# First mixer: the products of hv for token tile 1 put behind the first hu and hg, and conversions for the output projection put behind the subtraction of the mean

## The chip, the cores and the metric

The kernel runs on one core of one Trainium2 chip. The metric is the device time of one execution in microseconds (us). Five engines work side by side, each on its own queue in order: PE (TensorE: matmuls, with weight loads that overlap them), DVE (VectorE), ACT (ScalarE), POOL (GpSimd) and SP (SyncE, which here only issues transfers). An instruction waits at the head of its engine's queue until what it reads or overwrites is ready, and everything behind it on that engine waits too.

## The reference, cut to what matters

Two transformer layers on 256 tokens of width 1024 in float32, and then a third, different block. Each layer is a feed-forward (`swiglu`), a mixer, and a second feed-forward, each with a normalisation before and after it and a residual sum. The change touches the first layer's mixer and, through the order of conversions, the start of the feed-forward behind it:

```python
def even_mixer(h, w_in, w_out, dw_w, dw_b, ln_g, ln_b):
    q, k, v, u, gate = split(h @ w_in)        # 512 columns each
    a_out = stick_breaking_attention(q, k, v)  # 8 heads of 64
    c = u * sigmoid(gate)
    c = causal_depthwise_conv(c, dw_w, dw_b)   # 31 taps, 512 channels
    c = silu(layer_norm(c, ln_g, ln_b))        # mean and variance over the channels
    return concat([a_out, c]) @ w_out
```

## The kernel before, in words

All 256 tokens are in SBUF, in two token tiles of 128. A float32 product is made of three products of rounded parts: high by high, high by low, low by high. So every weight chunk of 512 KB is loaded by SP into one of four raw buffers, its high part is written by ACT (line 246, tile `hi`) and its low part by DVE (line 247, tile `lo`, raw minus hi; on POOL in a few places). That pair is called a conversion here. The chunks come in one fixed list, the plan, and are numbered here by their place in it: 66 to 69 are hv, 70 and 71 the first hu, 72 and 73 the first hg, 74 to 77 the second hu and hg, 78 to 85 hq and hk in turn, 86 to 93 ho (the output projection), and 94 to 97 the four chunks with which the next feed-forward starts.

`nxt` hands out the next chunks. Before that it converts ahead: up to `depth` chunks beyond the one in use, and at most one more than it hands out. With `ahead=False` it converts no more than what it hands out. `catch_up(n)` converts up to n more. For every name that `nxt` hands out it also calls the functions in the list `side`. Every order is the order of the program text; there is no planner.

At the end of a feed-forward, `boundary` adds its result to the residual, transposes token tile 0 for the next stage, writes its parts xh and xl (`evac`, lines 418 and 419), and makes one conversion (`catch_up(CU[1])`). The mixer then takes all four hv chunks and makes the products of token tile 0 with them; in between, token tile 1 is transposed, and after that its xh and xl are written, in the order k = 0, 4, 1, 5, 2, 6, 3, 7, its norm is taken, and two conversions are made (`catch_up(CU[2])`). Then come the products of token tile 1 (24 of 512 columns). Then `wp("hu")` and `wp("hg")`, 48 products of 256 columns each over both token tiles, `nz.rows()` (the norm as a row, `rb`, line 432), and on DVE `us` (841), `sgg` (845) and, after a sigmoid on ACT, the padded convolution input `cpad` (848), two channel blocks for each pass c of the loop at line 835.

The convolution has four channel blocks of 31 taps: blocks 0 and 2 on DVE (lines 798 to 805), blocks 1 and 3 as multiplies on ACT (808 to 821) and sums on POOL (818 to 823). `conv_some` is put into `side` after pass c = 0 and runs up to six times 3 or 2 DVE taps and 3 ACT taps with the hu, hg, hq and hk that follow. `qT` (863) and `kT` (866) are evacuated by DVE behind those taps. `z_` makes logits, `e_` their softplus (DVE end: `ze`, 892), `c_` the cumulative sums, `o_` the attention output. Behind the last `e_` the remaining DVE taps finish `y`; the first `part(HL, True)` of the output projection is called; PE sums `y` for the mean (924), DVE subtracts it (926), ACT squares, PE sums again for the variance (932), and the convolution's half of the output projection's input is made.

Of the kernel before, what the change touches and what calls it, by code (L numbers as in the profile page):

```python
# [12 lines left out]
AF = mybir.ActivationFunctionType  # L13
# [23 lines left out]
DEPTH = (14, (12, 9), (10, 10), (10, 10))  # L37
# [8 lines left out]
HL = ((1, 1),)  # L46
# [142 lines left out]
def block_kernel(ctx: ExitStack, tc: tile.TileContext, a: dict, out: bass.AP, upto: int = 99):  # L189
    nc = tc.nc  # L190
    pe, act, dve, pool = nc.tensor, nc.scalar, nc.vector, nc.gpsimd
# [20 lines left out]
    def s2(shape, dt=F32, name="s2"):  # L212
        return wk.tile(shape, dt, tag="s2", name=name, bufs=NS2)
# [4 lines left out]
    pos = {"dma": 0, "cv": 0, "use": 0, "depth": DEPTH[0]}  # L218
# [32 lines left out]
    def nxt(*names, ahead=True):  # L251

        i = pos["use"]
        for d_, nm in enumerate(names):
            assert plan[i + d_][0] == nm, (plan[i + d_][0], nm)
        n = i + len(names)
        feed_cv(max(n, min(i - 1 + pos["depth"], pos["cv"] + len(names) + 1)) if ahead else n)
        pos["use"] += len(names)
        for _ in names:
            for f in list(side):  # L260
                f()
        r = [cv_t.pop(i + d_) for d_ in range(len(names))]
        return r if len(r) > 1 else r[0]

    def catch_up(n, lo_on=dve):
        feed_cv(min(pos["use"] - 1 + pos["depth"], pos["cv"] + n), lo_on)

    def mm3(o, lh, ll, rh, rl, start, stop):
        pe.matmul(o, lh, rh, start=start, stop=False)  # L269
        pe.matmul(o, lh, rl, start=False, stop=False)  # L270
        pe.matmul(o, ll, rh, start=False, stop=stop)  # L271

    def tsl(t):
        return slice(t * 128, (t + 1) * 128)
# [277 lines left out]
    def smm(o, t, ch, k0, nk, xh, xl):  # L552
        for k in range(ch[0].shape[1]):
            kk = k0 + k
            mm3(o, xh[:, kk, tsl(t)], xl[:, kk, tsl(t)], ch[0][:, k], ch[1][:, k], kk == 0, kk == nk - 1)
# [5 lines left out]
            for t in range(2):  # L561
                smm(o(t), t, ch, k0, nk, xh, xl)

    def sproj_ab(o, name, xh, xl, nk=8, mid=None):

        chs = nxt(*[name] * (nk // 2), ahead=mid is None)
        for t in range(2):
            for i, ch in enumerate(chs):
                if t == 0 and i == nk // 2 - 1 and mid:
                    mid.trans(1, [0])  # L570
                smm(o(t), t, ch, 2 * i, nk, xh, xl)
            if t == 0 and mid:
                mid.trans(1, [1])
                mid.evac(1)
                mid.scale(1)
                catch_up(CU[2])

    def sproj_tail(name, xh, xl):

        f = [[None, None], [None, None]]  # L580
        pos["depth"] = DEPTH[0]
        todo = {t: {n: [0, 1, 2, 3] for n in range(2)} for t in range(2)}
        chs = {}

        def bank(t, n):
            f[t][n] = f[t][n] or pb()
            return f[t][n]

        def one(t, n, i):
            smm(bank(t, n), t, chs[i][n], 2 * i, 8, xh, xl)  # L590

        def part(leave=(), low_last=False):

            i = len(chs)
            chs[i] = nxt(name, name)
            tn = [(t, n) for t in range(2) for n in range(2) if (t, n) not in leave]
            for t, n in tn:
                todo[t][n].remove(i)
                if not low_last:
                    one(t, n, i)  # L600
            for low in range(2 if low_last else 0):
                for t, n in tn:
                    o = bank(t, n)
                    for k in range(2):
                        kk = 2 * i + k
                        hi, lo = (z[:, k] for z in chs[i][n])
                        if low:
                            pe.matmul(o, xl[:, kk, tsl(t)], hi, start=False, stop=kk == 7)
                        else:
                            pe.matmul(o, xh[:, kk, tsl(t)], hi, start=kk == 0, stop=False)  # L610
                            pe.matmul(o, xh[:, kk, tsl(t)], lo, start=False, stop=False)

        def pieces():
            i0 = len(chs)
            cs = nxt(*[name] * (2 * (4 - i0)), ahead=False)
            for i in range(i0, 4):
                chs[i] = cs[2 * (i - i0):2 * (i - i0) + 2]
            return lambda t: [(lambda n=n, i=i: one(t, n, i)) for n in range(2) for i in todo[t][n]]
        return f, part, pieces


    mod = const.tile([128, 48], F32, name="mod")
    part = const.tile([128, 192], F32, name="part")
# [142 lines left out]
    def even_mixer(nz):  # L766
        x = nz.x
        v = s4([128, 2, 512], name="v")
        pv = pp()
        sproj_ab(lambda t: pv[t], "hv", x.h, x.l, mid=nz)  # L770
        for t in range(2):
            act.activation(v[:, t], pv[t], AF.Copy, scale=x.r[t])
        cf, cr = s2([128, 3, 128], name="cf"), s2([128, 512], F32R, name="cr")
        ntri, nones, mean1 = cf[:, 0], cf[:, 1], cf[:, 2]
        idr, zmask = cr[:, :128], cr[:, 128:]
# [51 lines left out]
        def conv_some(n=None, m=TP):  # L827
            if n is None:
                n = TD[len(calls) % len(TD)]
                calls.append(n)  # L830
            for q, n_ in ((dq, n), (aq, m)):
                for _ in range(min(n_, len(q))):
                    tap(*q.pop(0))

        for c in range(2):
            pu = wp("hu", x)
            if c == 0:
                p = wp("hg", x)
                nz.rows()
            us = s2([128, 2, S], name="us")  # L840
            dve.tensor_tensor(us, two(pu), bc2(x.rb), op=ALU.mult)
            if c:
                p = wp("hg", x)
            sg = s2([128, 2, S], name="sgg")
            dve.tensor_tensor(sg, two(p), bc2(x.rb), op=ALU.mult)
            act.activation(sg, sg, AF.Sigmoid)
            for i in range(2):
                dve.tensor_tensor(cpad[2 * c + i][:, CW - 1:], sg[:, i], us[:, i], op=ALU.mult)
            dq += [(2 * c, k, True) for k in range(CW)]
            aq += [(2 * c + 1, k, False) for k in range(CW)]  # L850
            if c == 0:
                side.append(conv_some)
        pos["depth"] = DEPTH[1][1]
        act.preload_act_table_set("natural_log_exp_and_others")
        mh, ml = x8([128, 8, S], name="mh"), x8([128, 8, S], name="ml")
# [52 lines left out]
        def o_(hp):  # L908
            w = st.pop(hp)
            po = pb()  # L910
            for i in range(2):
                o = 64 * i
                hs = slice((2 * hp + i) * 64, (2 * hp + i + 1) * 64)
                pe.matmul(po[o:o + 64, 0:256], v[:, 0, hs], w[:, i, :256], start=True, stop=False)
                pe.matmul(po[o:o + 64, 128:256], v[:, 1, hs], w[:, i, 256:], start=False, stop=True)
            act.activation(mh[:, hp], po[:, :S], AF.Copy)
            dve.tensor_tensor(ml[:, hp], po[:, :S], mh[:, hp], op=ALU.subtract)
# [11 lines left out]
        def conv_var():  # L929
            pq.append(pb())  # L930
            for c in range(4):
                pe.matmul(pq[0][:, :S], mean1, y2[:, c], start=c == 0, stop=c == 3)
            rs = s2([128, S], name="rs")
            act.activation(rs, pq[0][:, :S], AF.Ln, bias=eps)
            act.activation(rs, rs, AF.Exp, scale=-0.5)
            act.preload_act_table_set("silu_and_others")
            t = s2([128, S], name="rst")
            dve.scalar_tensor_tensor(t, in0=pq[0][:, :S], scalar=EPS, in1=rs, op0=ALU.add, op1=ALU.mult)
            dve.scalar_tensor_tensor(t, in0=t, scalar=0.5, in1=rs, op0=ALU.mult, op1=ALU.mult)
            dve.scalar_tensor_tensor(rs, in0=t, scalar=1.5, in1=rs, op0=ALU.subtract, op1=ALU.mult, reverse0=True)  # L940
            for c in range(4):
                dve.tensor_tensor(y[:, c], y[:, c], rs, op=ALU.mult)
            for c in range(4):
                act.activation(y2[:, c], y[:, c], AF.Silu, scale=cols_[:, 2, 28 + c:29 + c],
                               bias=cols_[:, 2, 32 + c:33 + c])
                split_sb(mh[:, 4 + c], ml[:, 4 + c], y2[:, c])
# [18 lines left out]
        f, part, pieces = sproj_tail("ho", mh, ml)  # L965
# [1 line left out]
        conv_some(*TC[3])  # L967
        e_(3)
        conv_some(99, 99)
        part(HL, True)  # L970
        y2 = s4([128, 4, S], name="y2")
        c_(2)
        c_(3)
        conv_mean()
        o_(2)
        o_(3)
        conv_var()
        part(HL)
        return f, pieces()
# [565 lines left out]
    nz = Lazy(gcol(0, 0))  # L1545
# [19 lines left out]
    for i in range(6):  # L1565
# [8 lines left out]
        if i < 5:  # L1574
            l2, s2_ = divmod(i + 1, 3)
            nz = Lazy(gcol(l2, 2 * s2_))
        else:
# [4 lines left out]
            nz = Shifted(A1, mod[:, 0:8], fill)  # L1582
# [9 lines left out]
    nz = Shifted(A2, mod[:, 24:32], fill)  # L1592
# [46 lines left out]
```

## Time and profile before

| what | us |
|---|---|
| median of 3 runs | 1455.03 |
| lowest and highest run | 1448.93 and 1455.91 |
| profiled execution, its own time | 1453.46 |
| its span, first to last instruction | 1451.7 |
| PE busy in the span | 1432.5 |
| DVE busy in the span | 981.4 |
| ACT busy in the span | 758.4 |
| POOL busy in the span | 249.7 |

The span is what the trace shows; the execution's own time has some 1.8 us around it. The share of busy time is an average over stages: PE's few idle stretches are where time can be won or lost, and the mixer that the change touches lies between about 201 and 317 us of the span.

### The profile page before, as it was taken

The page shows a single profiled execution, that of the slowest core. Times are in us where ns is not written, and L with a number is a line of the kernel's source. Part 1 is how long each engine was busy: PE and PEld are TensorE (multiplying, and loading weights), DVE is VectorE, ACT ScalarE, POOL GpSimd, SP SyncE. Part 2 cuts the span into 40 slices and gives each one's busy share as a digit, 9 for nine tenths or more (in the row PEclk, how much of TensorE's full clock was granted, in tenths as well). Part 3 has the DMA queues.
Part 4 walks back from the last instruction along what each step waited for, and adds up shares of the span by engine and source line. Part 5 has one row for each costly group of instructions (what it writes and reads, how often), then busy time and mean ns, then how long its engine had stood idle before and what let it go on. Part 6 is the DMA issues. An engine that isn't in the chain of part 4 may idle for free.

```text
span 1451.7 us, 24310 instructions
## 1 busy us (share of the span) xinstructions
PE 1432.5 (99%) x9591; PEld 1308.9 (90%) x9591; DVE 981.4 (68%) x1348; ACT 758.4 (52%) x1166; POOL 249.7 (17%) x311
## 2 busy tenths in 40 slices
PE   9999999999999999999999999999999999999997
PEld 8899989789999999999898999998988877899997
DVE  5777667977777577765586777755695865575542
ACT  6544456965544464443664655445643665655431
POOL 3000023901100111000253100001232230200001
PEclk9999999999999999999999999999999999999999
DMA  8888645238887478775542587763664554387540
GB/s 267 265 270 250 200 145 168 73 117 285 270 264 232 146 256 268 224 233 161 172 145 65 184 292 251 236 193 111 206 202 132 188 168 143 116 270 239 176 129 29
DMA packets 194948, 281.03 MB, mean 194 GB/s; under 512 B 12381, under 2 KB 148241, under 8 KB 194834
## 3 DMA queue, kind: packets, MB, share of 16 engines
q1 hardware_dynamic: 184386, 248.87, 54.0%
q0 software_dynamic: 10048, 30.03, 6.3%
q8 instruction: 75, 1.23, 0.3%
q10 hardware_dynamic: 400, 0.57, 0.1%
q14 instruction: 39, 0.32, 0.1%
HBM read 277.90 MB, written 1.05 MB: 192 GB/s over the span
## 4 chain that ended last, share of the span: by engine, by line
PE 88%; DVE 5%; DMA 3%; ACT 2%; issue 1%; POOL 0%; SPq 0%; POOLq 0%; DVEq 0%; ACTq 0%
PE pb L269 27%; PE pb L271 26%; PE pb L270 26%; DVE lo L247 2%; DMA raw<-in_ffn_w_in_dram 2%; DVE pb L802 2%; PE pb L694 1%; PE pb L697 1%; PE pb L693 1%; PE pb L392 1%; ACT hi L246 1%; PE pb L1118 1%; DMA raw<-in_w_in_dram 0%; DMA raw<-in_ffn_w_out_dram 0%; PE pb L520 0%
## 5 line engine op out<-in xcount | busy, mean ns | idle before, releaser
L247 DVE TENSOR_TENSOR lo<-raw,hi 128x1024 fp32r<-128x1024 f32 (+1 forms) x461 | 551.6, 1224 | 239.9 <-ACT hi L246 203.4
L246 ACT ACTIVATE hi<-raw 128x1024 fp32r<-128x1024 f32 (+1 forms) x472 | 476.8, 1036 | 216.3 <-PE pb L271 68.1
L269 PE MATMUL pb<-xh,hi 128*128 128x256 f32 x1968 | 559.3, 284 | 2.7 <-DVE u L754 2.6
L271 PE MATMUL pb<-xh,lo 128*128 128x256 f32 x1968 | 557.8, 283 | 0.0
L270 PE MATMUL pb<-xl,hi 128*128 128x256 f32 x1968 | 557.8, 283 | 0.0
L269 PEld LDWEIGHTS pb<-xh,hi 128*128 128x128 f32 x1968 | 377.3, 192 | 6.0 <-issue 3.0
L270 PEld LDWEIGHTS pb<-xl,hi 128*128 128x128 f32 x1968 | 377.2, 192 | 2.0
L271 PEld LDWEIGHTS pb<-xh,lo 128*128 128x128 f32 x1968 | 377.3, 192 | 0.2
L269 PE MATMUL pb<-hi,hh 128*128 128x512 f32 x440 | 172.1, 391 | 0.0
L270 PE MATMUL pb<-lo,hh 128*128 128x512 f32 x440 | 171.8, 390 | 0.0
L271 PE MATMUL pb<-hi,hl 128*128 128x512 f32 x440 | 171.3, 389 | 0.0
L636 POOL DMA_DIRECT2D ada<-in_w_ada_dram x96 | 51.6, 541 | 455.2 <-PE pb L271 272.3
L527 ACT ACTIVATE hh<-u 128x512 fp32r<-128x512 f32 x50 | 31.6, 632 | 134.3 <-DVE u L754 134.3
L271 PEld LDWEIGHTS pb<-hi,hl 128*128 128x128 f32 x440 | 82.6, 188 | 17.5
L269 PEld LDWEIGHTS pb<-hi,hh 128*128 128x128 f32 x440 | 82.8, 188 | 15.8
L270 PEld LDWEIGHTS pb<-lo,hh 128*128 128x128 f32 x440 | 82.8, 188 | 15.4
L269 PE MATMUL pb<-hi,xh 128*128 128x512 f32 x224 | 90.8, 405 | 0.5 <-ACT xh L473 0.4
L271 PE MATMUL pb<-hi,xl 128*128 128x512 f32 x224 | 87.6, 391 | 0.0
L270 PE MATMUL pb<-lo,xh 128*128 128x512 f32 x224 | 87.4, 390 | 0.0
L739 ACT ACTIVATE sg<-sg 128x512 f32<-128x512 f32 x40 | 25.3, 632 | 111.8 <-DVE sg L738 111.8
L641 DVE SCALAR_TENSOR_TENSOR adacc<-ada,sc,adacc 128x512 f32<-128x512 f32 x84 | 63.0, 750 | 2.0
L754 DVE TENSOR_TENSOR u<-sg,pb 128x512 f32<-128x512 f32 x50 | 34.1, 682 | 40.3 <-PE pb L271 39.5
(322 smaller groups left out, 1652.2 us busy)
## 6 DMA issues: line engine op xcount, KB each, us to landing
raw<-in_ffn_w_in_dram SPq DMA_DIRECT2D x176, 512.0 KB, 5.1
raw<-in_ffn_w_out_dram SPq DMA_DIRECT2D x88, 512.0 KB, 4.6
raw<-in_w_in_dram SPq DMA_DIRECT2D x56, 512.0 KB, 4.1
ada<-in_w_ada_dram POOLq DMA_DIRECT2D x96, 256.0 KB, 4.4
raw<-in_gla_w_in_dram SPq DMA_DIRECT2D x24, 512.0 KB, 4.6
raw<-in_w_ffn_gate_dram SPq DMA_DIRECT2D x22, 512.0 KB, 4.6
raw<-in_w_ffn_up_dram SPq DMA_DIRECT2D x22, 512.0 KB, 4.9
raw<-in_w_ffn_down_dram SPq DMA_DIRECT2D x22, 512.0 KB, 4.1
```

Of the source, the lines that this page charges most:

```text
L246: act.activation(hv, r, AF.Copy)
L247: lo_on.tensor_tensor(lv, r, hv, op=ALU.subtract)
L269: pe.matmul(o, lh, rh, start=start, stop=False)
L270: pe.matmul(o, lh, rl, start=False, stop=False)
L271: pe.matmul(o, ll, rh, start=False, stop=stop)
L392: pe.transpose(nz.p[i][:, k * 128:(k + 1) * 128], h[:, t, c0:c0 + 128], ident)
L527: act.activation(hi, full, AF.Copy)
L636: pool.dma_start(t, w_ada[kt * 128:(kt + 1) * 128, cb * 512:(cb + 1) * 512])
L641: dve.scalar_tensor_tensor(ada["acc"], in0=t, scalar=sc[:, kt:kt + 1], in1=ada["acc"], op0=ALU.mult, op1=ALU.add)
L739: act.activation(sg, sg, AF.Silu)
L754: dve.tensor_tensor(u, sg, two(pb_), op=ALU.mult)
L802: dve.scalar_tensor_tensor(o, in0=src, scalar=w, in1=o, op0=ALU.mult, op1=ALU.add)
```

## The change: what it does

The mixer makes hv's products of token tile 0 as before, stops there, and makes those of token tile 1 only after the first hu, the first hg and the norm's row (`hv1()`). From the stop until then `depth` is 7. The convolution's first 5 DVE taps and 4 ACT taps are issued by themselves as soon as `cpad` 0 and 1 are made, and the two evacuations of v come behind them. At the mixer's end the first `part` of the output projection is called with `ahead=False`, so it converts nothing beyond what it uses, and one `catch_up(1)` is put behind `o_(3)`.

```diff
-    def sproj_ab(o, name, xh, xl, nk=8, mid=None):
+    def sproj_ab(o, name, xh, xl, nk=8, mid=None, later=False):
...
                 catch_up(CU[2])
+                if later:
+                    break
+
+        def rest():
+            for i, ch in enumerate(chs):
+                smm(o(1), 1, ch, 2 * i, nk, xh, xl)
+        return rest
...
-        def part(leave=(), low_last=False):
+        def part(leave=(), low_last=False, ahead=True):
             i = len(chs)
-            chs[i] = nxt(name, name)
+            chs[i] = nxt(name, name, ahead=ahead)
...
-        sproj_ab(lambda t: pv[t], "hv", x.h, x.l, mid=nz)
-        for t in range(2):
-            act.activation(v[:, t], pv[t], AF.Copy, scale=x.r[t])
+        hv1 = sproj_ab(lambda t: pv[t], "hv", x.h, x.l, mid=nz, later=True)
+        pos["depth"] = 7
...
                 p = wp("hg", x)
                 nz.rows()
+                hv1()
+                pos["depth"] = DEPTH[1][0]
...
             if c == 0:
                 side.append(conv_some)
+                conv_some(5, 4)
+                for t in range(2):
+                    act.activation(v[:, t], pv[t], AF.Copy, scale=x.r[t])
...
-        part(HL, True)
+        part(HL, True, False)
...
         o_(2)
         o_(3)
+        catch_up(1)
         conv_var()
         part(HL)
```

## Rows read from the trace of the kernel before

**Rows 1.** Page, busy us of an engine, share of the span, instructions.

```profile
PE 1432.5 (99%) x9591; PEld 1308.9 (90%) x9591; DVE 981.4 (68%) x1348; ACT 758.4 (52%) x1166; POOL 249.7 (17%) x311
```

**Rows 2.** Busy time by stretch: PE, PEld, DVE, ACT, POOL, clock, DMA share, GB/s.

```profile
278.00:290.00 12.00, 10.23 (x52) 7.26 (x52) 11.47 (x26) 11.87 (x23) 11.24 (x10) 1.00 0.00 0
```

**Rows 3.** PE's waits over the whole span: us, times, longest.

```profile
PE pb L269 <- DVE u L754: 2.6, 1, 2.6
...
PE pb L932 <- ACT y L927: 0.7, 1, 0.7
PE pb L875 <- DVE kT L866: 0.6, 1, 0.6
```

**Rows 4.** Timeline of PE: start, length, line, operation, tiles, count, wait before.

```profile
210.61 0.48 PE L269 MATMUL pb<-hi,xh 128*128 128x512 f32 x1
...
216.68 0.28 PE L269 MATMUL pb<-xh,hi 128*128 128x256 f32 x1
...
228.19 0.38 PE L430 MATMUL pb<-ident,rs_y 128*128 128x128 f32 x2
...
257.19 0.52 PE L871 MATMUL pb<-cr 128*128 128x384 f32 x2
...
281.31 1.53 PE L608 MATMUL pb<-hi,ml 128*128 128x512 f32 x6
...
291.64 1.99 PE L924 MATMUL pb<-y,cf 128*128 128x256 f32 x8 [0.22 <-DVE y L805]
```

**Rows 5.** Timeline of DVE up to the first convolution input.

```profile
213.65 0.35 DVE L419 SCALAR_TENSOR_TENSOR xl<-pb,cols,xh 128x128 fp32r<-128x128 f32 x1 [0.17 <-ACT xh L418]
...
230.31 0.42 DVE L432 COPY rb<-pb 128x256 f32<-128x256 f32 x1
...
234.09 0.76 DVE L848 TENSOR_TENSOR cpad<-sgg,us 128x256 f32<-128x256 f32 x2 [2.04 <-ACT sgg L846]
```

**Rows 6.** Timeline of ACT: four multiplies, v's evacuations, the table load.

```profile
216.63 1.25 ACT L772 ACTIVATE v<-pb,rs_y 128x512 f32<-128x512 f32 x2
...
236.75 1.70 ACT L816 ACTIVATE pt<-cpad,cols 128x256 f32<-128x256 f32 x4
...
247.69 1.28 ACT L854 ACT_TABLE_LOAD   x1
```

**Rows 7.** DVE's writes of lo from 214 to 231: ns, shortest, median, longest.

```profile
L247 DVE TENSOR_TENSOR lo<-raw,hi x7: 1218/1220/1226, 215.8 to 229.2; 128x1024 fp32r<-128x1024 f32 x7
```

**Rows 8.** Busy time of line 247 on DVE by stretch: DVE, clock, DMA share, GB/s.

```profile
238.00:271.00 33.00, 12.12 (x7) 1.00 0.38 123
```

**Rows 9.** Transfers of weight chunks issued from 180 to 260.

```profile
DMA to landing us min/median/max: 3.5/4.6/6.5
```

**Rows 10.** Timeline of DVE from the first taps to kT.

```profile
243.84 2.58 DVE L802 SCALAR_TENSOR_TENSOR pb<-cpad,cols,pb 128x256 f32<-128x256 f32 x5
...
248.38 2.58 DVE L802 SCALAR_TENSOR_TENSOR pb<-cpad,cols,pb 128x256 f32<-128x256 f32 x5
...
256.20 0.68 DVE L866 TENSOR_TENSOR kT<-pb,rb 128x512 f32<-128x512 f32 x1
```

**Rows 11.** Timeline of DVE from the last softplus to the mean's subtraction.

```profile
287.10 1.02 DVE L892 SCALAR_TENSOR_TENSOR ze<-pb,ze 128x384 f32<-128x384 f32 x2
...
291.50 3.49 DVE L247 TENSOR_TENSOR lo<-raw,hi 128x1024 fp32r<-128x1024 f32 x3
294.90 1.41 DVE L926 TENSOR_TENSOR y<-y,pb 128x256 f32<-128x256 f32 x4
```

**Rows 12.** Timelines of ACT, DVE and PE as the feed-forward starts.

```profile
319.32 1.04 ACT L246 ACTIVATE hi<-raw 128x1024 fp32r<-128x1024 f32 x1
...
321.35 1.22 DVE L247 TENSOR_TENSOR lo<-raw,hi 128x1024 fp32r<-128x1024 f32 x1
...
320.36 0.28 PE L694 MATMUL pb<-lo,xh 128*128 128x256 f32 x1
```

**Rows 13.** Busy time by stretch, as in rows 2, behind PE's longest wait.

```profile
68.00:70.00 2.00, 2.00 (x12) 2.00 (x10) 1.67 (x3) 1.98 (x3) 0.00 (x0) 0.50 0.50 163
```

## The prediction

> **What bounds the kernel now.** I read the page first: PE is busy for 99% of the span [rows 1], so an edit is worth what it does to PE's few waits. The list of those waits comes next: in the first mixer PE waits for `kT`, which DVE makes, and for the squares behind the subtraction of the mean [rows 3]. The table by stretch then says why: from 278 us to 290 DVE is busy for 11.5 of 12 us and ACT for 11.9, while PE falls to 10.2 [rows 2]. So in the mixer's second half DVE's queue, in its fixed order, sets when PE goes on; ACT and POOL are nearly as full. Ahead of that, to about 230 us, PE itself is the bound. The timelines give the places. In what follows a time is the start of the work in the trace of before, and "after" times are worked out from these durations.
>
> **hu ahead of hv's second half.** Before, the 24 products of 512 columns run from 210.61 to 216.68 [rows 4], 6.07 us, of which 24 times 0.228 (six such products take 1.53 [rows 4], five steps and the 0.39 of the last), 5.47, is work and 0.6 is waiting for token tile 1's xh and xl. After, hu takes that place. It uses up a k in 3 products of 0.12 us (hu and hg, 96 products, run from 216.68 to 228.19 [rows 4], 5.76 for each 48), and needs all of k = 0 to 3 first; xl is written in the order 0, 4, 1, 5, 2, 6, 3, 7 and its last one starts at 213.65 [rows 5], so k = 3 is there at about 213.5. From then the remaining 4.7 k of the first half take 1.7 us and the second half 2.9: hu ends at 218.1, not 216.4. That wait of 1.7 in place of 0.6 costs PE 1.1 us. Chunks 70 to 73 were converted before the mixer began, so nothing else holds hu and hg. hg ends at 223.85, against 228.19.
>
> **The convolution starts earlier.** Before, the copy of `rb` started only at 230.31, 2.1 us after its transposes, because DVE was still writing a lo; `cpad` was ready at 234.85 [rows 4, 5]. After, no conversion stands ahead of it (depth 7 allows none for hu or hg: with 78 already converted, the limit is 76 and then 78). The copy starts at 224.3, and the same 4.54 us of copy, products and sigmoid put `cpad` at 228.85: 6.0 us earlier.
>
> **What that costs.** The five conversions of chunks 78 to 82 ran on DVE between 222.9 and 230.4, at 1.22 us each with POOL idle [rows 7]. Now they come behind `cpad`, ahead of `kT`. The seven there took 12.12 us, 1.73 each [rows 8]. The walk of DVE from 228.85: 5 taps at 0.5 [rows 10] to 231.4; a wait for chunk 78's hi, which ACT reaches after four multiplies, the two moved evacuations of v [rows 6] and 1.0 of its own, at 232.8; three lo at 1.16, start to start, to 236.3; 5 taps and `us` to 239.4; three lo, POOL partly busy, 4.6, to 244.0; 5 taps, `sgg`, sigmoid and `cpad` as before (243.84 to 248.4 [rows 10]), to 248.6; a wait for hi, because ACT's table load [rows 6] has no multiplies behind it but conversions, to 250.0; two lo 2.5, 5 taps and `qT` 3.1, two lo beside a busy POOL 3.4, 5 taps and `kT` 3.1: `kT` at 262.1, against 256.8 [rows 10]. The ten lo cost 13.9 of that. All at 1.16 gives 259.9, all at 1.73 gives 265.5; I stand between because POOL has nothing to add until ACT has multiplied. The transfers for chunks 82 and on are issued when 78 and on are done; at 4.6 us to landing [rows 9] they arrive at about 238.6, when ACT wants them, and ahead of DVE.
>
> PE reaches the first logits at 223.85 + 0.13 + 5.47 for hv's rest + 5 times 5.76 = 258.3, against 257.19, where it did not wait [rows 4]. So it waits 3.8 us for `kT`. All DVE does from there to the last `ze` is the same and was back to back, so `kT`'s 5.3 us arrive at 288.12 [rows 11]. What was gained, five taps done early, is worth little: of six taps behind the last `ze` one is left, but PE's own work after that `ze` ended only 0.22 before `y` was there [rows 4]. The mean starts 5.1 us late.
>
> **Behind the mean.** Before, three lo (291.50 to 294.90) stood ahead of the subtraction [rows 11]; PE's sum, from 291.64 for 1.99 [rows 4], was done by 293.65. After, they are gone: the subtraction starts 1.2 us nearer to the mean. The variance's sum, for which PE waited 0.7 [rows 3], then stands behind `o_(2)` and `o_(3)` without a wait, so 0.7 is gained; the one conversion behind `o_(3)` ends on ACT about when Ln can start and on DVE about when Exp ends, which leaves 0.6.
>
> **What the lag costs later.** Conversions are now two fewer: 92, then 93 to 95, where before it was 92 to 97. Chunks 96 and 97, the second half of the feed-forward's first operands, are left for the boundary. The conversion there starts at 319.32 on ACT and at 321.35 on DVE, ending at 322.5, and the next follows to 323.7; PE's product with chunk 97's lo stood at 320.36 [rows 12]. PE waits 3.4 us, in a stage in which it never waits for the rest.
>
> **At nothing.** v's evacuations: first read by `o_(0)`, behind all of hq and hk; without that cover 1.25 us [rows 6]. Two PSUM banks and four chunks of hv are held 13 us longer: covered by banks and buffers that are read by then; if not, hu's second pass waits for v, 1.5 us, ahead of the wait for `kT`. Mask and constants: on SP and ACT where they were.
>
> **A rule beside this.** The seven lo beside POOL's adds took 1.73 us and the seven without 1.22 [rows 7, 8]. The Trainium skill (GPSIMD Engine Reference, Specifications) says that GpSimd's SBUF interfaces are shared with VectorE and contend with VectorE instructions of two SBUF inputs; the trace agrees. It speaks against this change: if all ten lo met a busy POOL, as an estimate by that page's rule at the trace's 1.73, the sum below would be 3.4 us higher.
>
> **Sum.** 5.1 - 0.6 + 3.4 = 7.9 us: 1453.46 becomes 1461.4. That execution lies 1.6 under the median of the runs; I add 0.6 for that to every case and forecast 1462.0. A change of 0.5% (7.3 us) is about what a measurement of this kernel can tell from none, so this stands on the edge of it.
>
> **Rivals.**
> - *The clock falls too.* PE's longest wait so far, 2.6 us [rows 3], was followed by a granted clock of 0.50, the lower of its levels (1.2 GHz in place of 2.4), all through the next stretch of 2 us [rows 13]: 1.0 us of PE lost there, at most 3.0 if both its neighbours were as low; I take 1.6. The waits for `kT` and for chunk 97 are as long. Behind the first, PE has 2 us to spare until `kT` of the second pass; behind the second it has none: 1463.6. Against it: the second is broken by some products at 322.5. The Trainium skill (TensorE: Matmul & The Clock Gate, Part 1) says that the throttled state is the default and activity releases it; the trace agrees.
> - *ACT runs ahead, DVE is in time (not slower).* If ACT's conversions come before its multiplies give POOL work, the ten lo cost 11.6 and DVE waits for no hi: 25 taps 12.5, lo 11.6, the rest 3.1, so `kT` at 256.1. It decides at 29.5 us from `cpad` to `kT` (228.85 to PE's 258.3); I have 33.2. Then the mean is 0.2 early, and with -0.6 and the boundary's 3.4 there is +2.6: 1456.7. For it: seven lo in a row did take only 1.22 while POOL was idle [rows 7]. Against: v's evacuations and the table load stand ahead of the conversions.
> - *The feed-forward's front is hidden.* If chunks 96 and 97 are ready in time, 4.5 us remain: 1458.6. I see no cover.
> - *The edit does what its order suggests.* Taps 6 us early, DVE ahead for good, PE's 1.8 us without work in one stretch [rows 2], some 3 with those beside it, gone: about 1451.
>
> **Numbers.** Forecast 0.38, clock 0.20, ACT ahead 0.20, hidden front 0.12, early taps 0.06, something faster still 0.04. Range 1454.0 to 1466.0: from just under ACT ahead to the clock with most lo at 1.73; the likeliest alone is 1459.5 to 1464.5. Slower by over 0.5% are 0.6 of the forecast's case and nearly all of the clock's, 0.42; faster by over 0.5% 0.04; within it 0.54.
>
> **What would show it.** `cpad` ends near 228.9 and `kT` near 262; PE waits for `kT` ahead of line 871 by 2 to 5 us; the mean near 296.7 with the subtraction right behind; in the feed-forward PE waits 3 us for lo at line 694. The prediction is wrong if DVE covers `cpad` to `kT` in under 29.5 us, or if PE does not wait at 694.

## The result, and the profile after

The changed kernel took 1461.34 us in the median of 6 runs, the kernel before 1452.53 us in 6: the ratio is 1.0068, with a 95% interval of 1.0055 to 1.008. It is slower by 8 to 12 us, a little over the 0.5% that a measurement can tell from no change, and inside the range.

The two profiled executions differ before they reach the change: the last write of token tile 1's xl starts at 213.65 in the one [rows 5] and at 209.28 in the other, although every instruction to there is the same. So from here on a place in the program is given in us from that write, which is the last one that the kernels share. The timeline of DVE in the changed kernel:

```profile
209.28 0.35 DVE L419 SCALAR_TENSOR_TENSOR xl<-pb,cols,xh 128x128 fp32r<-128x128 f32 x1 [0.17 <-ACT xh L418]
...
219.98 0.42 DVE L432 COPY rb<-pb 128x256 f32<-128x256 f32 x1 [6.17 <-PE pb L430]
...
223.77 0.76 DVE L856 TENSOR_TENSOR cpad<-sgg,us 128x256 f32<-128x256 f32 x2 [2.04 <-ACT sgg L854]
...
228.55 3.50 DVE L247 TENSOR_TENSOR lo<-raw,hi 128x1024 fp32r<-128x1024 f32 x3 [1.47 <-ACT hi L246]
...
235.05 5.35 DVE L247 TENSOR_TENSOR lo<-raw,hi 128x1024 fp32r<-128x1024 f32 x3
...
246.57 2.36 DVE L247 TENSOR_TENSOR lo<-raw,hi 128x1024 fp32r<-128x1024 f32 x2 [1.61 <-ACT hi L246]
...
251.94 4.22 DVE L247 TENSOR_TENSOR lo<-raw,hi 128x1024 fp32r<-128x1024 f32 x2
...
258.56 0.68 DVE L877 TENSOR_TENSOR kT<-pb,rb 128x512 f32<-128x512 f32 x1
...
292.29 0.42 DVE L811 TENSOR_TENSOR y<-y,pb 128x256 f32<-128x256 f32 x1
296.93 1.42 DVE L937 TENSOR_TENSOR y<-y,pb 128x256 f32<-128x256 f32 x4 [4.22 <-PE pb L935]
```

The copy of rb waits for PE alone, and `cpad` ends at 15.3 in place of 21.2 [rows 5]: 5.9 us earlier. Then come ten subtractions in four groups, two of them behind a wait for ACT, and `kT` starts at 49.3 in place of 42.6 [rows 10]. Between the end of `y` and the mean's subtraction DVE stands idle for 4.2 us and waits for PE's sum. POOL's sums, from its timeline, stand beside the second and the fourth of these groups:

```profile
231.35 4.61 POOL L824 TENSOR_TENSOR ya<-ya,pt 128x512 f32<-128x512 f32 x3 [3.56 <-ACT pt L822]
237.62 5.31 POOL L824 TENSOR_TENSOR ya<-ya,pt 128x512 f32<-128x512 f32 x3 [1.67 <-ACT pt L822]
248.43 11.54 POOL L824 TENSOR_TENSOR ya<-ya,pt 128x512 f32<-128x512 f32 x7 [5.49 <-ACT pt L822]
```

The timeline of PE:

```profile
259.30 1.65 PE L886 MATMUL pb<-qT,kT 64*128 64x256 f32 x8 [4.72 <-DVE kT L877]
...
295.00 1.89 PE L935 MATMUL pb<-y,cf 128*128 128x256 f32 x8
...
323.01 0.38 PE L700 MATMUL pb<-hi,xh 128*128 128x256 f32 x1 [0.38 <-ACT hi L246]
325.22 0.44 PE L701 MATMUL pb<-lo,xh 128*128 128x256 f32 x1 [1.82 <-DVE lo L247]
...
326.36 0.58 PE L701 MATMUL pb<-lo,xh 128*128 128x256 f32 x1 [0.27 <-DVE lo L247]
...
342.57 0.38 PE L430 MATMUL pb<-ident,rs_y 128*128 128x128 f32 x2
```

The first logits wait 4.72 us for `kT`, where they had not waited [rows 4]; the sum for the mean starts at 85.7 in place of 78.0 [rows 4]; and the feed-forward waits for the hi of chunk 96, its lo, and the lo of chunk 97. The last row is the feed-forward's own row of the norm, the end of what the change disturbs: at 133.3. In the kernel before the same row of PE's timeline is at 121.7:

```profile
335.38 0.38 PE L430 MATMUL pb<-ident,rs_y 128*128 128x128 f32 x2
```

The busy time by stretch in the changed kernel shows PE and, third from the end, its granted clock:

```profile
256.00:258.00 2.00, 0.00 (x0) 0.00 (x0) 1.90 (x5) 2.00 (x6) 1.92 (x2) 0.79 0.77 221
...
264.00:266.00 2.00, 2.00 (x11) 2.00 (x11) 1.86 (x5) 1.94 (x3) 0.00 (x0) 0.50 0.65 207
266.00:268.00 2.00, 2.00 (x14) 2.00 (x14) 2.00 (x6) 2.00 (x4) 0.00 (x0) 0.65 0.20 77
...
326.00:328.00 2.00, 1.73 (x8) 1.65 (x8) 0.30 (x1) 0.00 (x0) 0.00 (x0) 0.50 0.70 185
```

The clock fell to its lower level (1.2 GHz) behind both waits. By these stretches it stood there for 10.2 us, from 257.2 to 267.4, of which PE worked for 8.1 (from 259.3 on), and again for 3.4 us around 326.

### The profile page after: what moved, and what is told of

It reads as the page before. It is cut to its first block, busy times and chain, and to the rows that moved or that the text cites. A ratio compares the mean times of both kernels' runs of the same rounds, so it can differ in the third digit from the quotient of the medians.

```text
span 1460.2 us, 24308 instructions
## 1 busy us (share of the span) xinstructions
PE 1436.1 (98%) x9591; PEld 1310.3 (90%) x9591; DVE 984.2 (67%) x1348; ACT 759.4 (52%) x1166; POOL 251.3 (17%) x311
## 4 chain that ended last, share of the span: by engine, by line
PE 86%; DMA 4%; DVE 4%; ACT 4%; issue 1%; POOL 0%; SPq 0%; POOLq 0%; DVEq 0%; ACTq 0%
PE pb L269 26%; PE pb L270 26%; PE pb L271 26%; DMA raw<-in_ffn_w_in_dram 3%; DVE lo L247 2%; DMA raw<-in_ffn_w_out_dram 2%; ACT hi L246 1%; PE pb L701 1%; PE pb L704 1%; PE pb L700 1%; PE pb L392 1%; DVE pb L808 1%; PE pb L1130 1%; ACT pt L822 1%; PE pb L886 0%
## 5 line engine op out<-in xcount | busy, mean ns | idle before, releaser
L527 ACT ACTIVATE hh<-u 128x512 fp32r<-128x512 f32 x50 | 31.6, 632 | 130.9 <-DVE u L761 130.9
```

The lines of the kernel that those rows point to most:

```text
L527: act.activation(hi, full, AF.Copy)
```

## The experiments

In 5 to 12 runs each, against the kernel before on the same chip. Two theories stand: the loss is DVE's lateness to `kT`, made by conversions and taps that now stand ahead of it, plus the feed-forward's front; or it lies in the new order of products, in v's evacuations, or at the front alone. All places in us from the shared write, read from the timelines of each profile:

| kernel | cpad done | kT starts | mean | transposes for the feed-forward | its norm row | ratio (95%) |
|---|---|---|---|---|---|---|
| before | 21.2 | 42.6 | 78.0 | 100.0 | 121.7 | 1 |
| after | 15.3 | 49.3 | 85.7 | 106.9 | 133.3 | 1.0068 (1.0055 to 1.008) |
| first edit alone | 15.3 | 49.3 | 84.7 | 105.9 | 127.6 | 1.0041 (1.0029 to 1.0053) |
| second edit alone | 22.0 | 43.3 | 78.4 | 99.6 | 126.4 | 1.0033 (1.0021 to 1.0046) |
| second edit, front fed | 21.9 | 43.2 | 78.3 | 99.5 | 123.7 | 1.0031 (1.0019 to 1.0043) |
| after, front fed | 15.3 | 49.3 | 84.5 | 105.7 | 131.3 | 1.0057 (1.0044 to 1.007) |
| after, PE filled | 15.3 | 49.3 | 84.1 | 105.3 | 130.5 | 1.0102 (1.0086 to 1.0118) |
| after, no early taps | 15.3 | 46.1 | 83.0 | 104.3 | 130.9 | 1.0045 (1.0032 to 1.0059) |
| after, depth 9 | 17.0 | 47.4 | 83.0 | 104.3 | 129.5 | 1.0059 (1.0047 to 1.0072) |
| after, v late | 15.3 | 48.4 | 84.2 | 105.5 | 130.8 | 1.0061 (1.0049 to 1.0074) |
| three taken back | 17.0 | 41.8 | 77.7 | 99.7 | 121.5 | 0.9982 (0.9971 to 0.9993) |
| depth 7 alone | 19.5 | 47.9 | 83.0 | 105.0 | 126.8 | 1.0033 (1.0021 to 1.0045) |
| early taps alone | 21.9 | 46.9 | 82.7 | 103.9 | 125.6 | 1.0022 (1.0007 to 1.0037) |

**The first edit alone**

```diff
-        part(HL, True, False)
+        part(HL, True)
...
         o_(3)
-        catch_up(1)
```

> The first edit alone: hv's second half behind hu and hg, early taps, v behind them; the output projection converts ahead as before. Theory (DVE comes late to kT, and the lag of two conversions is paid at the feed-forward's front): only the mixer's part is left, 5 to 7 us over the kernel before, ratio 1.0035 to 1.005; PE still waits 4 to 5 us for kT, and no longer for lo of chunk 97. Rival (the whole loss is at the feed-forward's front): within 1 us of before, 0.9995 to 1.0005. Rival (the conversions taken from the front of the subtraction are what kept the loss small): as slow as the whole change or slower, 1.007 or more.

As the theory said: 1.0041. The transposes come 5.9 us late and nothing is lost after them (21.8 us to the norm's row, as before). PE waits for `kT` as in the whole change. Both rivals fall. One thing I had not expected is in its DVE timeline:

```profile
293.66 3.49 DVE L247 TENSOR_TENSOR lo<-raw,hi 128x1024 fp32r<-128x1024 f32 x3
297.96 1.42 DVE L937 TENSOR_TENSOR y<-y,pb 128x256 f32<-128x256 f32 x4 [0.82 <-PE pb L935]
```

The three subtractions in front of the mean's subtraction cost nothing here. The early taps end y before PE has finished its part, and they fit into that time.

**The second edit alone**

```diff
-        part(HL, True)
+        part(HL, True, False)
...
         o_(3)
+        catch_up(1)
```

> The second edit alone on the kernel before: the output projection's first part converts nothing ahead, one conversion behind the last attention output. Theory: the subtraction of the mean comes 0.6 us earlier, and PE then waits 3.4 us for chunks 96 and 97 at the feed-forward's front, with 1 us more if the granted clock falls: 2.8 to 4 us over before, ratio 1.002 to 1.003. Rival (the front is hidden): 0.6 us faster, 0.9996.

1.0033, a little above the range. From the mean to the transposes it wins 0.8 us (21.2 in place of 22.0), and from the transposes to the norm's row it loses 5.1 (26.8 in place of 21.8). The front is not hidden.

**The front fed, with the change and with the second edit alone**

```diff
-PRT = ((0, 0, 0), (1, 0, 0))
+PRT = ((0, 0, 2), (1, 0, 0))
```

The third number of the first group is how many conversions `boundary` makes behind the mixer between its two halves, with their lo on POOL.

> The changed kernel, with chunks 96 and 97 converted between the two halves of the boundary (hi on ACT in a stretch in which it was idle for 2 us, lo on POOL). Theory: the wait at the feed-forward's front goes, with the clock's fall behind it: 4 to 5 us under the changed kernel, ratio to before 1.003 to 1.0045, and no wait of PE at the line of the lo products. Rival (PE's wait there only takes up lateness that comes out elsewhere): as the changed kernel, 1.0068.

> The kernel before with the second edit and with the two conversions given back between the halves of the boundary. Theory: the subtraction's 0.6 us without its price: 0.6 us under before, ratio 0.9992 to 1.0. Rival (the conversions cost as much wherever they stand): 1.001 or more.

PE no longer waits at the lo products, but only 0.7 of 4.6 us came back with the change (25.7 from the transposes to the norm's row) and 2.6 of 5.1 with the second edit alone (24.2). The timelines of PE, DVE and POOL in the latter show the new wait:

```profile
312.75 0.63 PE L392 MATMUL pb<-ident,h 128*128 128x128 f32 x4 [2.21 <-DVE h L363]
```

```profile
306.94 2.89 DVE L363 SCALAR_TENSOR_TENSOR h<-tm,rs_y,h 128x512 f32<-128x512 f32 x1 [0.66 <-POOL rs_y L331]
...
310.46 2.14 DVE L363 SCALAR_TENSOR_TENSOR h<-tm,rs_y,h 128x512 f32<-128x512 f32 x1
...
318.04 0.75 DVE L363 SCALAR_TENSOR_TENSOR h<-tm,rs_y,h 128x512 f32<-128x512 f32 x1 [0.66 <-POOL rs_y L331]
```

```profile
306.88 5.18 POOL L247 TENSOR_TENSOR lo<-raw,hi 128x1024 fp32r<-128x1024 f32 x2
```

With the two subtractions on POOL, DVE's addition to the residual took 2.89 and 2.14 us beside them and 0.75 without. Taken singly, the subtractions end at 309.28 and 312.06, and each addition ends 0.5 us behind one of these. The transposes wait for that sum. So my expectation fell: the front's wait was replaced by another, through the very contention that the prediction weighed for the lo.

Part of the 2.6 us that came back is the clock, which fell at the front in the second edit's execution and did not in the fed one. Like for like, feeding the front is worth less: 0.7 us between the two executions in which it fell (26.4 and 25.7), and 1.0 against executions further down in which it did not (25.2 and 24.2).

**PE filled**

```diff
             p = wp("hq", x)
+            if mid:
+                d = pb()
+                for _ in range(36):
+                    pe.matmul(d[:, :S], x.h[:, 0, :128], x.h[:, 1], start=True, stop=True)
             for f in mid:
```

> The changed kernel with 36 extra products of 256 columns (4.3 us of PE) into a spare bank ahead of the first logits, where PE waits 4.7 us for kT; they add work that the output does not use. Theory with the clock: kT comes when it came, PE's wait shrinks to about 0.5 us, the granted clock stays at its upper level, the second pass of hk ends 3 us earlier and the mixer 1.5 to 2 us earlier: ratio to before 1.005 to 1.006. Rival (the clock's fall there is covered by DVE's lateness, as predicted): as the changed kernel, 1.0068. Rival (the bound there is PE): 4 us slower than the changed kernel, 1.0095.

In the mixer it went as the theory with the clock said: `kT` at the same 49.3, the wait mostly gone, and the clock at its upper level through it. PE's timeline, and the stretches:

```profile
266.09 0.92 PE L890 MATMUL pb<-qT,kT 64*128 64x256 f32 x8 [0.39 <-DVE kT L881]
```

```profile
264.00:266.00 2.00, 1.70 (x14) 1.38 (x12) 1.93 (x5) 2.00 (x5) 1.84 (x3) 1.00 0.87 237
266.00:268.00 2.00, 1.91 (x14) 1.47 (x16) 2.00 (x3) 0.99 (x4) 1.92 (x2) 1.00 0.07 26
```

The mean comes 1.7 us earlier than in the changed kernel, in spite of 4.3 us of work that nobody needs, so PE is not the bound there. Yet the whole was slower, 1.0102, which is near the figure of that rival. The loss lies in stages that the edit does not touch: the shared write itself came at 216.06 in place of 209.28, and PE's waits over the span name two places far from the mixer, 3.7 us in the first feed-forward and 2.8 in the third block (0.5 and 1.3 in the changed kernel):

```profile
PE pb L269 <- DVE u L761: 3.7, 1, 3.7
PE pb L1307 <- DVE rt L1351: 2.8, 1, 2.8
```

The first of these is also where the kernel before waited 2.6 us [rows 3]. In four of the thirteen profiled executions (before, second edit alone, depth 9, PE filled) PE waits there for 2.1 to 3.7 us, with the clock at 0.50 behind it, and these four reach the shared write at 213.0 to 216.1. In the other nine it waits 0.9 us or less, and they reach it at 208.8 to 211.3. Why `u` comes late in those four was not settled. The timed ratio of this kernel says nothing about the mixer.

**No early taps; depth 9; v late**

```diff
-                conv_some(5, 4)
```

```diff
-        pos["depth"] = 7
+        pos["depth"] = 9
```

```diff
         qk(0)
+        for t in range(2):
+            act.activation(v[:, t], pv[t], AF.Copy, scale=x.r[t])
         qk(1, [z01])
```

(the two lines of the last are taken from behind the early taps)

> The changed kernel without the 5 DVE taps and 4 ACT taps that are issued by themselves; they run at the end of the convolution instead. Theory (what DVE does ahead of kT sets PE): kT comes 2 to 2.6 us earlier, PE waits for it 2 to 2.7 us in place of 4.7, and the taps cost nothing at the end, where PE's own work behind the last ze is as long: 2 to 4 us under the changed kernel, ratio to before 1.004 to 1.0055. Rival (early taps are what the change gains): 1.0068 or more, the mean later.

> The changed kernel with depth 9 in place of 7 while hu and hg run, so that chunks 78 and 79 are converted with the first hg, in the stretch in which DVE is idle for 6 us and POOL too. Theory: two subtractions of 1.2 us leave the way to kT; kT 2 to 3.5 us earlier, ratio to before 1.003 to 1.0055. Rival (their buffers come free too late, so that the copy of rb waits behind them): the first convolution input later by 1 to 2 us and no gain, 1.006 to 1.008.

> The changed kernel with v's two evacuations put behind the first hq and hk, away from the front of chunk 78's conversion. Theory (DVE's own work is the bound, its waits for ACT are small): hi of chunk 78 comes 1.2 us earlier and kT 1 to 1.4 us earlier, ratio to before 1.0055 to 1.0065. Rival (ACT's order sets DVE's): kT 3 us or more earlier, 1.005 or less. Rival (v's place is nothing): 1.0068.

`kT` came 3.2, 1.9 and 0.9 us earlier, and the mean with it, 2.7, 2.7 and 1.5. Each time the transposes followed. The gains at the mean hold the clock too: it stood at 0.50 for 10.2 us behind `kT` in the changed kernel's execution, for 6.8 in those of depth 9 and v late, and in the one without early taps it fell only later, for 3.4 us just ahead of the mean. The first `kT` gained more than forecast (2 to 2.6) and the other two a little less (2 to 3.5, 1 to 1.4). The taps cost more than their own 2.5 us: without them the ten lo took 13.2 us, from start to start, instead of 15.1, because ACT's early multiplies also start POOL's sums: the second group of three took 3.5 us in place of 5.35, and POOL's sums stood beside it only at its end. With depth 9 the wait of rb's copy that the rival named is there (`cpad` 1.7 us later), and yet `kT` gains. v's place is worth about what was forecast. The ratio of depth 9, 1.0059, is a little above its range. By the timed ratios the last two are within each other's intervals and the changed kernel's.

**Three taken back**

The three edits above in one kernel, with the second edit undone.

> The first edit's order of products (hv's second half behind hu and hg) with three things taken from the way to kT at once: no early taps, depth 9 so that two chunks are converted with the first hg, v's evacuations behind the first hq and hk; the output projection converts ahead as before. Theory (DVE's work between the first cpad and kT is the whole of the mixer's loss): the single gains of 3.2, 1.9 and 0.9 us add up, kT comes within 1 us of where it stood before, PE does not wait for it, and what is left is hu's wait for xl, about 1 us: ratio to before 0.9995 to 1.0012. Rival (the reordering of the products itself costs PE 3 us or more): 1.002 or more. Rival (with DVE relieved the earlier cpad pays): 0.998 or less.

Its DVE timeline:

```profile
220.72 2.36 DVE L247 TENSOR_TENSOR lo<-raw,hi 128x1024 fp32r<-128x1024 f32 x2 [5.65 <-ACT hi L246]
223.00 0.42 DVE L432 COPY rb<-pb 128x256 f32<-128x256 f32 x1
...
252.28 0.68 DVE L874 TENSOR_TENSOR kT<-pb,rb 128x512 f32<-128x512 f32 x1
```

The three gains add up to 5.9 us and measured 7.5: `kT` is 0.8 us ahead of the kernel before, PE does not wait for it, and the transposes stand at 99.7, where they stood before. hv's second half is still behind hu and hg. So the order of the products costs nothing by itself, and the mixer's whole loss lies in what stands ahead of `kT`. hu's wait for xl does move the first logits by 1.2 us, but PE waited for DVE later anyway. The ratio, 0.9982, is below one and below the range that I gave; up to the feed-forward's norm row the trace shows only 0.25 us of that. The rest lies where the two kernels are the same: its 12 runs lie between 1448.63 and 1451.26 us, the 29 of the kernel before between 1449.32 and 1456.87. So I don't call this version faster.

**Depth 7 alone, early taps alone, on the kernel before**

```diff
+        pos["depth"] = 7
         for t in range(2):
             act.activation(v[:, t], pv[t], AF.Copy, scale=x.r[t])
...
                 nz.rows()
+                pos["depth"] = DEPTH[1][0]
```

```diff
                 side.append(conv_some)
+                conv_some(5, 4)
```

> The kernel before, its products and evacuations in their old order, with depth 7 alone while the first hu and hg run: the five conversions of chunks 78 to 82 fall behind the first cpad. Theory (the lost look-ahead is the loss): cpad comes 2 us earlier, since no subtraction stands ahead of rb's copy, and kT 4 to 6.5 us later; PE waits for it 4 to 6 us: 4 to 6.5 us over before, ratio 1.0028 to 1.0045. Rival (look-ahead is hidden, products and taps cost): within 1 us of before, 0.9993 to 1.0007.

> The kernel before with nothing but the 5 DVE and 4 ACT taps issued by themselves behind the first cpad. Theory: kT 2.5 us later, PE waits for it about 2 us and gets back 0.4 at the mean: 1.5 to 2.2 us over before, ratio 1.001 to 1.0016, near what a measurement can tell; the trace tells it. Rival (early taps shorten the convolution): the mean earlier than before.

The lost look-ahead alone makes `kT` 5.4 us late and the transposes 5.0, 1.0033: most of the first edit's loss with none of its reordering. DVE's timeline and PE's wait:

```profile
224.74 0.42 DVE L432 COPY rb<-pb 128x256 f32<-128x256 f32 x1 [10.44 <-PE pb L430]
...
257.70 0.68 DVE L868 TENSOR_TENSOR kT<-pb,rb 128x512 f32<-128x512 f32 x1
```

```profile
PE pb L877 <- DVE kT L868: 4.6, 1, 4.6
```

DVE is idle for 10.4 us ahead of rb's copy, which is where the five conversions had stood. The early taps alone cost more than forecast: `kT` 4.4 us late in place of 2.5 and the transposes 3.9, since the lo beside POOL's sums grew by 1.0 us and `cpad` itself came 0.7 later in that execution.

## Why the prediction was right, step by step

- *hu ahead of hv's second half.* The norm's row after hg was forecast for 10.2 us from the shared write (223.85) and came at 10.3. The 1.1 us that this costs PE are real and were covered, as the kernel with three things taken back shows.
- *The convolution's start.* 15.2 forecast, 15.3 measured, with the copy of rb free of conversions.
- *`kT`.* 47.9 forecast (its start), 49.3 measured. From start to start the ten lo cost 15.1 us where I had 13.9, and the waits for hi were 1.47 and 1.61 against 1.4 each. The price of a lo beside POOL's sums pointed the right way: of the ten, four took 2.0 to 2.3 us, all in the groups of 5.35 and 4.22 that stood beside POOL's sums, and six took 1.2.
- *From `kT` to the mean.* Forecast 5.1 us late; measured 7.7, and 6.1 with PE kept busy. This is the term that was mis-sized, by 2.6 us. 1.4 of that is `kT`. The rest is the clock: I had said that PE has 2 us to spare behind the first wait. In the changed kernel the clock stood at 0.50 for 10.2 us there, and the mean came 1.7 us later than with PE kept busy. Two other executions have the same `kT` and the same wait of 4.72 us. With the first edit alone the clock stood at 0.50 for 6.8 us and the mean lost 0.7; with the front fed it was 3.4 us and 0.4. The busy time by stretch, first edit alone and then front fed:

```profile
260.00:262.00 2.00, 0.67 (x4) 0.59 (x6) 1.97 (x4) 1.20 (x3) 1.92 (x2) 0.58 0.67 247
...
266.00:268.00 2.00, 2.00 (x15) 2.00 (x14) 1.86 (x5) 1.94 (x4) 0.00 (x0) 0.72 0.72 203
```

```profile
258.00:260.00 2.00, 0.69 (x4) 0.61 (x6) 1.97 (x4) 0.57 (x2) 1.90 (x2) 0.88 0.61 238
260.00:262.00 2.00, 2.00 (x10) 1.25 (x10) 2.00 (x2) 1.13 (x3) 1.86 (x2) 0.50 0.01 4
262.00:264.00 2.00, 2.00 (x15) 1.71 (x14) 1.93 (x4) 1.97 (x4) 1.32 (x1) 0.77 0.66 244
```

- *Behind the mean.* Forecast 0.6 us gained; 0.8 measured from the mean to the transposes. But the first edit alone shows the same 0.8, and so do the early taps alone (21.2 in place of 22.0). With the early taps in place the second edit added nothing there, and the early taps, which I had called worth little, are worth this. The step had the right size and the wrong owner.
- *The feed-forward's front.* Forecast 3.4 us. Of the six executions with the second edit and an unfed front, three show 3.5 (25.2 in place of 21.8): PE filled, depth 9 and v late, with the clock at 1.00 throughout. The other three show 4.6 to 5.1: the changed kernel, the second edit alone and no early taps, each with the clock at 0.50 for 3.4 us there, the fall that I had as a rival. Behind the norm's row the changed kernel's execution lost another 1.3 us by the end of its span; I leave that open. Ten of the thirteen executions, the kernel before among them, take 1116.2 to 1116.6 us from that row to the end.
- *The sum.* 7.9 us forecast; from the shared write to the norm's row 11.6 us in the profile, 2.6 of the difference up to the mean and 1.2 at the front. Between the medians it is 8.8. That the time itself, 1461.34, came within 1 us of the forecast's 1462.0 is partly luck: the execution of the kernel before from which I started had reached the shared write 4.4 us later than the changed kernel's, behind its wait of 2.6 us in the first feed-forward [rows 3]. The forecast and the rival with the clock both came true in part.

Of the rivals, ACT running ahead fell: DVE took 34.7 us from `cpad` to the end of `kT`, against 29.5 at which it decides. The hidden front fell, and so did the taps that pay.

## What to carry to other kernels

Moving a product later does not only move its time: here it came with a shorter look-ahead (depth 7), and the work that look-ahead had put into an idle stretch fell behind the next consumer, which alone made up most of the mixer's loss. Before issuing work early on an engine that is the bound, ask which result that engine owes to PE next and count what now stands ahead of it. And look at a gain twice when two edits aim at one place: here the early taps or the second edit, each alone, won the same 0.8 us. Where executions differ by as much as the effect, time a stage from the last instruction that the kernels share.

## What the runs showed of the hardware that I had not expected

An addition of two SBUF tensors on DVE that takes 0.75 us took 2.89 and 2.14 beside POOL's subtractions: an operation handed to POOL to relieve DVE cost DVE 3.5 us. The Trainium skill (GPSIMD Engine Reference, Specifications) names this contention, of GpSimd with VectorE instructions of two SBUF inputs; the trace agrees with it. The granted clock stayed at 0.50 for 10.2, 6.8 and 3.4 us behind the same wait of 4.72 in three executions, with PE at work again. Kernels whose instructions are the same up to a place reached it at 208.8 to 216.1 us in their profiled executions, which is as much as the whole effect studied here, and the late ones are those in which PE had waited more than 2 us for one result in the first feed-forward.
